# Seven half-size products for u and z of a gMLP layer, sums of weights on GpSimd, y kept where v was

## The chip, the cores and the metric

The kernel runs on one core of one Trainium2 chip. The metric is the device time of one execution in microseconds (us). A core has a matrix engine (TensorE, PE in the profile; its loads of stationary operands are PEld), a vector engine (VectorE, DVE), a scalar engine (ScalarE, ACT), GpSimd (POOL), and queues that start DMA transfers (here almost all on SyncE, SP). Each engine takes its instructions in a fixed order and waits on semaphores for the others.

## The reference, cut to what matters

Two layers work on 512 prompt rows and 128 sample rows (640 tokens, five tiles of 128). Layer 0 is a gMLP, layer 1 an attention layer; after each stand an output product, a norm and a gated embedding. The change is in the gMLP:

```
def gmlp_branch(h, w_in, ln_g, ln_b, w_s, b_s, w_out):
    proj = h @ w_in                      # 640 x 1024 times 1024 x 6144
    uv = gelu(proj[..., :2 * E])         # E = 2048
    z = proj[..., 2 * E:]
    u = uv[..., :E]
    v = layer_norm(uv[..., E:], ln_g, ln_b)
    s = einsum('gij,bnjgc->bnigc', masked w_s, v blocks) + b_s     # 16 groups of 128 columns
    y = u * s * silu(z)
    return y @ w_out, v
```

Everything is float32.

## The kernel before, in words

Every float32 operand of a large product is split in two (`split`): `hi` is a rounded copy made by ScalarE, `lo = x - hi` is made by VectorE. A product is then three matmuls, `mm3`: hi·hi, hi·lo, lo·hi. The input h (normed, transposed) lies split in the tile `A`, as `h_hi` and `h_lo`, eight blocks k of 128 rows by 640 tokens.

Weights come in units of 512 KB, 128 x 1024 on chip. `fetch` starts their DMA into one of three slots of `RAW`; `prefetch` splits a unit into one of five slots of `W`; `weights(n)` hands out the next n units and lets `prefetch` run as far ahead as slots allow. A unit's split waits until the matmuls that read its slot's old content are done.

The gMLP has two stages. The **v stage** makes v token-major: four panels p of 512 columns, in each four units, five token tiles. ScalarE applies the gelu to each bank of PSUM and VectorE gathers the statistics (`bn_stats`). `layer_norm_panel(p)` then takes two VectorE operations for each of five tiles. The **u/z stage** goes through 16 groups g of 128 channels, channel-major. For each pair of groups one weight pair gives u and one gives z: `channel_unit` runs over the eight k, each with two pieces of tokens (384 and 256) of three matmuls. ScalarE takes u out of PSUM with a gelu; z goes through a tanh on ScalarE and one VectorE operation. Then come, for each group, the gate `tz = 0.5 * tz * u`, the weights of the spatial product (`spatial_weights`: a multiply on VectorE, two transposes, three copies on ScalarE), the spatial matmuls on v, two additions of the bias on VectorE out of PSUM, and `y = s * tz`. All eight PSUM banks go round in one ring.

The output product (`tail`) splits y and runs over units of `w_out`.

The program order below is only a proposal: a scheduler at compile time sets each engine's order from its own estimate of when work is ready. Work that is written later can stand earlier on an engine.

Of the kernel before, what the change touches and what calls it, by code (L numbers as in the profile page):

```python
# [10 lines left out]
F32 = mybir.dt.float32  # L14
# [6 lines left out]
P = 128  # L21
# [5 lines left out]
NB = 8  # L27
# [26 lines left out]
def hybrid_trunk(tc, x_prompt, x_sample, ck, cv, clf, p_prompt, p_sample, norm_pre, norm_post,  # L54
# [56 lines left out]
    def dma(out, in_):  # L111
        nc.sync.dma_start(out=out, in_=in_)
# [30 lines left out]
    u_tail(f_wout, 1)  # L143


    n0 = 48 + 16 + 2 + 8
    few = range(n0, n0 + 64 + 12)
    slots, last_use = {}, [-1] * NW
    state = {"raw": 0, "used": 0}

    def raw_of(i):
        o = (i % NRAW) * 1024
        return RAW[:, o:o + 1024]

    def fetch(upto):
        while state["raw"] < min(upto, len(units)):
            ap, k = units[state["raw"]]
            dma(raw_of(state["raw"]).rearrange("p (k n) -> p k n", k=k), ap)
            state["raw"] += 1

    def prefetch(upto, i0=0):

        while len(slots) < min(upto, len(units)):
            i = len(slots)
            taken = {slots[k] for k in range(i0, i)}
            free = [z for z in range(NW - (i in few)) if z not in taken]
            if not free:
                return
            z = min(free, key=lambda z: last_use[z])
            slots[i], last_use[z] = z, i  # L170
            fetch(i + 1)
            split(W[:, z * 2048:z * 2048 + 1024], W[:, z * 2048 + 1024:z * 2048 + 2048], raw_of(i))

    def weights(n):

        i0 = state["used"]
        state["used"] += n
        prefetch(i0 + NW, i0)
        res = []
        for i in range(i0, i0 + n):  # L180
            k, o = units[i][1], slots[i] * 2048
            res.append(tuple(W[:, o + z:o + z + 1024].rearrange("p (k n) -> p k n", k=k) for z in (0, 1024)))
        return res

    def mm3(out, lhs, rhs, start, stop):
        (lh, ll), (rh, rl) = lhs, rhs
# [76 lines left out]
    def channel_unit(ws, hh, banks):  # L263
        return run(channel_steps(ws, hh, banks))

    def interleave(steps, pieces):

# [52 lines left out]
        prefetch(t + 1)  # L320


    def v_at(p, t):
        return r1(p * 2560 + t * 512, 512)

    stats = [small(24, keep=True) for _ in range(NT)]
    for p in range(4):
        out = [bank((0, 1, 2, 3, 4, 5, 6, 7)) for _ in range(NT)]
        for kk in range(4):
            (w,) = weights(1)  # L330
            for t in range(NT):
                for j in range(2):
                    k = 2 * kk + j
                    mm3(out[t], h_at(k, t * P, (t + 1) * P), (w[0][:, j], w[1][:, j]), k == 0, k == 7)
        for t in range(NT):
            nc.scalar.activation(out=v_at(p, t), in_=out[t], func=AF.Gelu_apprx_tanh)
            nc.vector.bn_stats(out=stats[t][:, 6 * p:6 * p + 6], in_=v_at(p, t))
    for p in range(4):
        dma(r2(6144 + p * 1024, 512), ln_g[0, p * 512:(p + 1) * 512].partition_broadcast(P))
        dma(r2(6144 + p * 1024 + 512, 512), ln_b[0, p * 512:(p + 1) * 512].partition_broadcast(P))  # L340
    mu, rs = [], []
    for t in range(NT):
        mv = small(2, keep=True)
# [15 lines left out]
    w16 = r1(o_A, 256).rearrange("p (g j) -> p g j", g=16)  # L359
    for b in range(NB):  # L360
        dma(w16[b * TS:(b + 1) * TS], w_s[0, :, :TS, :TS].rearrange("g i j -> i g j"))
    for z in range(2):
        nc.gpsimd.memset(r1(o_wm + z * P, P)[64:128, 0:64], 0.0)

    def spatial_weights(g):
# [7 lines left out]
        b = bank()  # L373
# [12 lines left out]
    for g in range(16):
        if g == 0:
            layer_norm_panel(2)
        if g == 2:
            layer_norm_panel(3)  # L390
        if g % 2 == 0:
            wz = weights(2)
            for i in range(2):
                for (a, b), o in zip(SPLITS, channel_unit(wz, i, (0, 1, 2, 3, 4, 5, 6, 7))):
                    nc.scalar.activation(out=uv_of(g + i)[0][:, a:b], in_=o[:, :b - a], func=AF.Gelu_apprx_tanh)
            wz = weights(2)
# [14 lines left out]
        nc.tensor.matmul(b1[:, :P], v_at(pnl, 4)[:, c0:c0 + P], ws, start=True, stop=True)  # L411
        nc.vector.tensor_tensor(
            out=tmp[:, :512].rearrange("p (t i) -> p t i", t=4), in0=b0.rearrange("p (t i) -> p t i", t=4),
            in1=bs.unsqueeze(1).broadcast_to([P, 4, P]), op=ALU.add)
        nc.vector.tensor_tensor(
            out=tmp[:, 512:].rearrange("p (t i) -> p t i", t=NB), in0=b1[:, :P].rearrange("p (t i) -> p t i", t=NB),
            in1=bs[:, :TS].unsqueeze(1).broadcast_to([P, NB, TS]), op=ALU.add)
        nc.vector.tensor_tensor(out=tmp, in0=tmp, in1=tz, op=ALU.mult)


    def tail(layer, y_at, first_banks, attention=None):
# [541 lines left out]
```

## Time and profile before

| | |
|---|---|
| three timed runs | 1358.04, 1358.42, 1358.46 us (median 1358.42) |
| profiled execution | 1358.35 us, its span 1356.5 us |
| TensorE busy | 1345.5 us, 99% of the span |
| VectorE busy | 661.0 us, 49% |
| ScalarE busy | 492.1 us, 36% |
| GpSimd busy | 33.6 us, 2% |
| DMA | 170.73 MB, mean 126 GB/s |

The span is what the trace covers; 1.85 us of the execution lie around it. A busy share is a mean over stages with different limits. A matmul's duration in the trace is longer than its distance to the next one, since matmuls are pipelined; the distance from start to start is what counts. The u/z stage lies between about 126 and 373 us.

### The profile page before, as it was taken

What the parts mean: (1) busy time and instruction counts of PE and PEld (TensorE: products, weight loads), DVE (VectorE), ACT (ScalarE), POOL (GpSimd) and SP (SyncE); (2) the same over time, 40 slices, a digit from 0 to 9 for tenths busy, and PEclk for the clock granted to TensorE, in tenths of its full rate; (3) what the DMA queues carried; (4) which work ended last, traced back from release to release, by engine and by line L of the source; (5) the groups of instructions that cost most, each with busy time, mean ns of one, the idle gap of its engine ahead of it and who ended that gap; (6) DMA issues with size and microseconds to landing.
All of it is one profiled execution on the core that took longest, in us unless ns stands there. A gap on an engine that the chain in (4) does not pass through costs nothing.

```text
span 1356.5 us, 21525 instructions
## 1 busy us (share of the span) xinstructions
PE 1345.5 (99%) x8553; PEld 1221.1 (90%) x8553; DVE 661.0 (49%) x1435; ACT 492.1 (36%) x954; POOL 33.6 (2%) x80
## 2 busy tenths in 40 slices
PE   8999999999999999999999999999999999999998
PEld 6888999999988878899999999999999999788786
DVE  7335833343454364644545444554545465544642
ACT  5232222222335343533333333333433344445331
POOL 1000000000000010100000000000000000000100
PEclk8999999999999999999999999999999999999999
DMA  8322332322232213578888676775888587444111
GB/s 280 126 78 65 117 108 80 132 72 73 65 110 78 79 45 83 146 168 164 145 143 173 151 156 153 164 161 126 137 153 171 144 205 225 132 124 132 63 62 47
DMA packets 296983, 170.73 MB, mean 126 GB/s; under 512 B 188450, under 2 KB 266786, under 8 KB 296883
## 3 DMA queue, kind: packets, MB, share of 16 engines
q1 hardware_dynamic: 296738, 169.10, 50.2%
q8 instruction: 67, 1.10, 0.3%
q14 instruction: 34, 0.27, 0.1%
q10 hardware_dynamic: 144, 0.26, 0.1%
HBM read 147.75 MB, written 21.58 MB: 125 GB/s over the span
## 4 chain that ended last, share of the span: by engine, by line
PE 98%; DVE 1%; DMA 0%; ACT 0%; issue 0%; SPq 0%; POOL 0%; DVEq 0%
PE pb L187 29%; PE pb L189 29%; PE pb L188 29%; PE pb L778 3%; PE pb L771 1%; PE pb L832 1%; PE pb L225 1%; PE pb L858 1%; PE pb L410 1%; PE pb L855 1%; DMA RAW<-in_gmlp_w_in 0%; PE pb L850 0%; PE pb L411 0%; PE pb L749 0%; PE pb L865 0%
## 5 line engine op out<-in xcount | busy, mean ns | idle before, releaser
L187 PE MATMUL pb<-A,W 128*128 128x256 f32 (+1 forms) x1280 | 410.3, 321 | 0.0
L189 PE MATMUL pb<-A,W 128*128 128x256 f32 (+1 forms) x1280 | 397.0, 310 | 0.0
L188 PE MATMUL pb<-A,W 128*128 128x256 f32 (+1 forms) x1280 | 395.9, 309 | 0.0
L202 DVE TENSOR_TENSOR W<-RAW,W 128x1024 fp32r<-128x1024 f32 x164 | 200.4, 1222 | 255.2 <-ACT W L201 253.3
L187 PE MATMUL pb<-W,A 128*128 128x512 f32 (+1 forms) x840 | 297.8, 355 | 3.6 <-ACT A L201 2.2
L189 PE MATMUL pb<-W,A 128*128 128x512 f32 (+1 forms) x840 | 293.4, 351 | 0.3 <-DVE A L202 0.3
L188 PE MATMUL pb<-W,A 128*128 128x512 f32 (+1 forms) x840 | 293.6, 350 | 0.0
L201 ACT ACTIVATE W<-RAW 128x1024 fp32r<-128x1024 f32 x164 | 173.0, 1055 | 209.9 <-PE pb L188 106.2
L187 PEld LDWEIGHTS pb<-A,W 128*128 128x128 f32 x1280 | 241.5, 189 | 7.5 <-issue 6.8
L188 PEld LDWEIGHTS pb<-A,W 128*128 128x128 f32 x1280 | 241.3, 189 | 0.6
L189 PEld LDWEIGHTS pb<-A,W 128*128 128x128 f32 x1280 | 240.9, 188 | 0.5 <-issue 0.4
L187 PEld LDWEIGHTS pb<-W,A 128*128 128x128 f32 x840 | 159.0, 189 | 27.6 <-issue 3.1
L189 PEld LDWEIGHTS pb<-W,A 128*128 128x128 f32 x840 | 158.9, 189 | 20.9 <-DVE A L202 0.7
L188 PEld LDWEIGHTS pb<-W,A 128*128 128x128 f32 x840 | 159.0, 189 | 20.2 <-issue 0.4
L810 DVE STREAM_TRANSPOSE r2b_t<-r2b_t 128x256 f32<-128x256 f32 x128 | 46.0, 411 | 30.0 <-PE pb L832 26.7
L773 ACT ACTIVATE R<-pb 128x128 f32<-128x128 f32 (+1 forms) x64 | 28.0, 437 | 65.8 <-PE pb L771 65.6
L202 DVE TENSOR_TENSOR A<-r2a_t,A 128x640 fp32r<-128x640 f32 x32 | 25.0, 821 | 45.3 <-ACT A L201 45.2
L778 PE MATMUL pb<-R 128*128 128x128 f32 x320 | 46.2, 275 | 0.0
L778 PEld LDWEIGHTS pb<-R 128*128 128x128 f32 x320 | 41.5, 191 | 0.8 <-issue 0.4
L201 ACT ACTIVATE A<-r2a_t 128x640 fp32r<-128x640 f32 x32 | 22.7, 740 | 47.4 <-PE pb L188 46.7
L712 DVE SCALAR_TENSOR_TENSOR R<-R,pb 128x384 f32<-128x384 f32 (+1 forms) x32 | 14.8, 484 | 44.5 <-ACT R L711 44.4
L211 POOL TENSOR_TENSOR SML<-SML 128x1 f32<-128x1 f32 x25 | 19.3, 770 | 694.0 <-DVE SML L209 579.4
(198 smaller groups left out, 1386.5 us busy)
## 6 DMA issues: line engine op xcount, KB each, us to landing
RAW<-in_fox_w_in SPq DMA_DIRECT2D x64, 512.0 KB
RAW<-in_gmlp_w_in SPq DMA_DIRECT2D x48, 512.0 KB
r2b_t<-in_cache_fox_v SPq DMA_DIRECT2D x32, 512.0 KB
r2b_t<-in_cache_fox_k SPq DMA_DIRECT2D x128, 128.0 KB
RAW<-in_gmlp_w_out SPq DMA_DIRECT2D x16, 512.0 KB
RAW<-in_ple_w_gate SPq DMA_DIRECT2D x16, 512.0 KB
RAW<-in_fox_w_out SPq DMA_DIRECT2D x16, 512.0 KB
out<-R SPq DMA_DIRECT2D x40, 128.0 KB
```

What stands on the lines that cost most here:

```text
L187: nc.tensor.matmul(out, lh, rh, start=start, stop=False)
L188: nc.tensor.matmul(out, lh, rl, start=False, stop=False)
L189: nc.tensor.matmul(out, ll, rh, start=False, stop=stop)
L201: nc.scalar.activation(out=hi, in_=src, func=AF.Copy)
L202: nc.vector.tensor_tensor(out=lo, in0=src, in1=f(hi), op=ALU.subtract)
L211: nc.gpsimd.tensor_tensor(out=q, in0=t, in1=mhalf, op=ALU.pow)
L225: nc.tensor.transpose(out=b[:, j * P:(j + 1) * P], in_=src[:, (4 * c + j) * P:(4 * c + j + 1) * P], identity=ident)
L410: nc.tensor.matmul(b0[:, t * P:(t + 1) * P], v_at(pnl, t)[:, c0:c0 + P], wm, start=True, stop=True)
L712: nc.vector.scalar_tensor_tensor(out=tz[:, a:b], in0=tz[:, a:b], scalar=1.0, in1=ps[:, :b - a], op0=ALU.add, op1=ALU.mult)
L773: nc.scalar.activation(out=pt[:, :n], in_=tb[:, :n], func=AF.Copy)
L778: nc.tensor.matmul(O[:, d], v[:, j, hh * P:(hh + 1) * P], pt[:, j * P:(j + 1) * P], start=(j == 0), stop=(j == i))
L810: nc.vector.transpose(out=kt[:, hh, bl, :PAST], in_=kr[:, hh, bl])
```

## The change

u and z of a pair of groups (256 channels by 640 tokens, 1024 deep) are no longer made by eight half-size products (two halves of channels, two of tokens, two of depth) but by seven, in Strassen's way (Winograd's form). A half-size product has 128 channels, 320 tokens and a depth of 512: four k, three matmuls each, 12 matmuls.

- **Right operands** (from h): four sums of quarters of h. `right_operands` makes them once, on VectorE, in the v stage: four additions hi + lo and four subtractions of 128 x 1280, and three splits into a new tile `TB`; the fourth is split into the place of a quarter of h that nothing reads after (`split(*quarter(0, 1), b12)`).
- **Left operands** (from weights): `left_operands` makes four sums of quarters of the two weight units, 128 x 512 each, on GpSimd, into the tile `SF`, which has room for one set. So each set of seven needs four splits in place of two: one of 512 columns and three of 1024. `W` is handed out in ten half slots. A fourth slot for raw weights (`o_X`) is added.
- **Results**: `seven_products` puts each product into one of four banks (`UZ`); the other four (`SPA`) serve the spatial part. One product is copied by ScalarE; each of the other six is taken out of PSUM by VectorE additions, seven in all for each set (L485, L495, L497, L500). The gelu and the tanh then read SBUF.
- **y in place of v**: y of group g is written over the columns of v that it was made from (`y0_at`); the place that y had is used by `TB` and `SF`. Gain and bias of the layer norm are loaded panel by panel into one place (`load_ln`), and the norm of panels 1 to 3 is written between the groups.

```
+    def left_operands(i, j):
+        (a11, a21), (a12, a22) = ([raw_of(r).rearrange("p (k n) -> p k n", k=4)[:, :, z:z + P] for z in (0, P)] for r in (i, i + 1))
+        s2, s3, s1, s4 = (SF[:, z * 512:z * 512 + 512].rearrange("p (k n) -> p k n", k=4) for z in range(4))
+        if j == 0:
+            for o, a, b, op in ((s1, a21, a22, ALU.add), (s2, s1, a11, ALU.subtract), (s3, a11, a21, ALU.subtract),
+                                (s4, a12, s2, ALU.subtract)):
+                nc.gpsimd.tensor_tensor(out=o, in0=a, in1=b, op=op)
+        return (a11, SF[:, :1024], SF[:, 1024:2048], raw_of(i + 1))[j]
...
+    def right_operands():
+        for q, (i, j) in zip((b11, b12, b21, b22), ((0, 0), (0, 1), (1, 0), (1, 1))):
+            hi, lo = quarter(i, j)
+            nc.vector.tensor_tensor(out=q, in0=f(hi), in1=f(lo), op=ALU.add)
+        for o, a, b, dst in ((t_a, b12, b11, 0), (t_b, b22, t_a, 1), (b21, b21, t_b, 2), (b12, b22, b12, None)):
+            nc.vector.tensor_tensor(out=o, in0=a, in1=b, op=ALU.subtract)
+            if dst is not None:
+                split(*right_sum(dst), o)
...
+            if (p, kk) == (0, 1):
+                right_operands()
+            if (p, kk) == (3, 1):
+                split(*quarter(0, 1), b12)
...
+    UZ = (0, 1, 2, 3)
+    def seven_products(into, done):
+        rights = (quarter(0, 0), right_sum(1), quarter(0, 1), right_sum(0), quarter(1, 1), quarter(1, 0), right_sum(2))
+        def total(i, j, a, b):
+            nc.vector.tensor_tensor(out=into(i, j), in0=a, in1=b, op=ALU.add)
+            done(i, j, into(i, j))
+        for n, (w, right) in enumerate(zip(seven_left(), rights)):
+            o = bank(UZ)[:, :HT]
+            for k in range(4):
+                mm3(o, (w[0][:, k], w[1][:, k]), (right[0][:, k], right[1][:, k]), k == 0, k == 3)
+            if n == 0:
+                nc.scalar.activation(out=m1, in_=o, func=AF.Copy)
+            elif n == 1:
+                nc.vector.tensor_tensor(out=u2, in0=m1, in1=o, op=ALU.add)
+            elif n == 2:
+                nc.vector.tensor_tensor(out=u3, in0=u2, in1=o, op=ALU.add)
+            elif n == 3:
+                total(1, 1, u3, o)
+                nc.vector.tensor_tensor(out=u2, in0=u2, in1=o, op=ALU.add)
+            elif n == 4:
+                total(0, 1, u2, o)
...
-        tmp = r2(g * TOK, TOK)
-        for (a, b), o in zip(SPLITS, channel_unit(wz, g % 2, (0, 1, 2, 3, 4, 5, 6, 7))):
-            nc.scalar.activation(out=tz[:, a:b], in_=o[:, :b - a], func=AF.Tanh, scale=0.5)
-            nc.vector.scalar_tensor_tensor(out=tz[:, a:b], in0=tz[:, a:b], scalar=1.0, in1=o[:, :b - a], op0=ALU.add, op1=ALU.mult)
...
+    for g in range(0, 16, 2):
+        for part, finish in ((0, finish_u), (1, finish_z)):
+            if 2 * part in SEVEN:
+                seven_products(lambda i, j: uv_of(g + i)[part][:, HALF[j]], lambda i, j, c: finish(g, i, j, c))
+            else:
+                eight_products(lambda i, j, c: finish(g, i, j, c))
+        if g < 12:
+            layer_norm_panel(1 + g // 4, range(3) if g % 4 == 0 else range(3, NT))
+        for i in range(2):
+            gate_spatial(g + i)
```

What the change does to the order of the engines shows at the beginning of the u/z stage. On VectorE before, at the first groups of z, stand the last operations of the layer norm (L352, L353), the tanh's product that frees a bank of z (L401), splits of weights (L202) and the spatial part (L370, L412, L415); `pb_71` is PSUM bank 1, `R_69` the tile that holds v, u, tz and the rest.

```order
L353 SCALAR_TENSOR_TENSOR R_69<-R_69,SML,r2a_t 128x512 x2
L401 SCALAR_TENSOR_TENSOR R_69<-R_69,pb_71 128x384
L353 SCALAR_TENSOR_TENSOR R_69<-R_69,SML,r2a_t 128x512
L401 SCALAR_TENSOR_TENSOR R_69<-R_69,pb_72 128x256
L370 TENSOR_TENSOR R_69<-CST,R_69 128x128
L202 TENSOR_TENSOR W<-RAW,W 128x1024
L401 SCALAR_TENSOR_TENSOR R_69<-R_69,pb_76 128x384
```

On VectorE now, at the end of the first set of seven (u of groups 0 and 1) and the start of the second, the sums that free the four banks (L485, L500) stand between the layer norm of panels 1 and 2 (L435, L436), the bias additions of the first groups (L525, L527) and splits (L251).

```order
L251 TENSOR_TENSOR W<-RAW,W 128x1024
L435 SCALAR_TENSOR_TENSOR R_69<-R_69,SML 128x512 x5
L485 TENSOR_TENSOR R_69<-R_69,pb_73 128x320
L500 TENSOR_TENSOR R_69<-R_69,pb_73 128x320
L485 TENSOR_TENSOR R_69<-R_69,pb_71 128x320
L458 TENSOR_TENSOR R_69<-CST,R_69 128x128
L525 TENSOR_TENSOR R_69<-pb_76,R_69 128x4x128
L525 TENSOR_TENSOR R_69<-pb_75,R_69 128x4x128
L436 SCALAR_TENSOR_TENSOR R_69<-R_69,SML 128x512 x2
L485 TENSOR_TENSOR R_69<-R_69,pb_72 128x320
```

In the program panel 1 is normed after the sets of u and z; on VectorE its five first operations now stand ahead of the sums of the fourth product (bank 3, rows three and four), and so ahead of the release of the banks that the second set needs.

On GpSimd before, nothing but the small powers of the norms (L211) stands here. Now the sums of weights (L185) of the second and third set stand around the five powers of the layer norm (L260).

```order
L185 TENSOR_TENSOR sf<-R_69 128x512 [waits DMAHW6_49,DVE_49]
L185 TENSOR_TENSOR sf<-R_69,RAW 128x512 [waits DMAHW6_49,DMAHW3_49,DVE_49]
L185 TENSOR_TENSOR sf<-sf,R_69 128x512 [waits Pool_49]
L185 TENSOR_TENSOR sf<-RAW,sf 128x512 [waits Pool_49]
L260 TENSOR_TENSOR SML<-SML 128x1 [waits DVE_49] x3
L185 TENSOR_TENSOR sf<-RAW 128x512 [waits DMAHW7_49,DVE_49]
L260 TENSOR_TENSOR SML<-SML 128x1 [waits DVE_49] x2
L185 TENSOR_TENSOR sf<-RAW 128x512 [waits DMAHW1_49,DVE_49]
```

The last two powers, which the norm of tiles 3 and 4 needs, now stand behind a sum that waits for a split on VectorE.

## Rows read from the trace of the kernel before

**Rows 1.** Profile page: span, busy times, the chain that ended last.
```profile
span 1356.5 us, 21525 instructions
...
PE 1345.5 (99%) x8553; PEld 1221.1 (90%) x8553; DVE 661.0 (49%) x1435; ACT 492.1 (36%) x954; POOL 33.6 (2%) x80
...
PE 98%; DVE 1%; DMA 0%; ACT 0%; issue 0%; SPq 0%; POOL 0%; DVEq 0%
```
**Rows 2.** Windows: us, busy us (instructions) of PE, PEld, DVE, ACT, POOL, granted clock, DMA.
```profile
0.00:36.00 36.00, 31.48 (x133) 23.84 (x134) 25.82 (x52) 18.05 (x30) 3.98 (x11) 0.91 0.85 285
36.00:126.00 90.00, 90.00 (x399) 74.53 (x398) 30.48 (x36) 25.16 (x31) 0.99 (x1) 1.00 0.29 92
126.00:373.00 247.00, 247.00 (x1720) 246.91 (x1719) 120.61 (x190) 70.82 (x149) 3.94 (x4) 1.00 0.28 89
```
**Rows 3.** Windows of 10 and 20 us in the u/z stage; VectorE third.
```profile
126.00:136.00 10.00, 10.00 (x69) 9.91 (x68) 10.00 (x20) 2.96 (x7) 0.99 (x1) 1.00 0.03 8
...
156.00:166.00 10.00, 10.00 (x76) 10.00 (x75) 9.09 (x17) 2.74 (x7) 0.00 (x0) 1.00 0.68 230
...
286.00:306.00 20.00, 20.00 (x140) 20.00 (x140) 5.32 (x9) 4.95 (x11) 0.00 (x0) 1.00 0.20 62
```
**Rows 4.** Timeline of PE, u/z stage's start and middle: start, us, instruction.
```profile
126.33 0.42 PE L187 MATMUL pb<-A,W 128*128 128x384 f32 x1
...
302.68 0.27 PE L374 MATMUL pb<-CST,R 128*128 128x128 f32 x1
...
303.93 0.42 PE L187 MATMUL pb<-A,W 128*128 128x384 f32 x1
...
304.89 0.33 PE L187 MATMUL pb<-A,W 128*128 128x384 f32 x1
...
308.42 0.34 PE L187 MATMUL pb<-A,W 128*128 128x384 f32 x1
```
**Rows 5.** Groups by line and form, VectorE: count, busy us, mean ns.
```profile
L202 DVE TENSOR_TENSOR W<-RAW,W 128x1024 fp32r<-128x1024 f32 x164 | 200.4, 1222 | 255.2 <-ACT W L201 253.3 <-DMA out<-R 0.5
...
L202 DVE TENSOR_TENSOR W<-R,W 128x512 fp32r<-128x512 f32 x32 | 21.9, 686 | 0.4 <-ACT W L201 0.4
...
L353 DVE SCALAR_TENSOR_TENSOR R<-R,SML,r2a_t 128x512 f32<-128x512 f32 x20 | 13.9, 744 | 0.0
...
L402 DVE SCALAR_TENSOR_TENSOR R<-R 128x640 f32<-128x640 f32 x16 | 13.1, 820 | 0.2
...
L401 DVE SCALAR_TENSOR_TENSOR R<-R,pb 128x384 f32<-128x384 f32 x16 | 8.8, 548 | 4.9 <-ACT R L400 4.9
...
L401 DVE SCALAR_TENSOR_TENSOR R<-R,pb 128x256 f32<-128x256 f32 x16 | 6.6, 412 | 0.0
```
**Rows 6.** Timeline of VectorE and GpSimd where both are at work.
```profile
5.48 0.56 POOL L211 TENSOR_TENSOR SML<-SML 128x1 f32<-128x1 f32 x1 [4.51 <-DVE SML L209]
...
123.60 2.73 DVE L352 SCALAR_TENSOR_TENSOR R<-R,SML,r2a_t 128x512 f32<-128x512 f32 x4
...
123.77 0.99 POOL L211 TENSOR_TENSOR SML<-SML 128x1 f32<-128x1 f32 x1 [97.64 <-DVE SML L207]
...
486.37 1.21 DVE L202 TENSOR_TENSOR W<-RAW,W 128x1024 fp32r<-128x1024 f32 x1
486.53 1.48 POOL L211 TENSOR_TENSOR SML<-SML 128x1 f32<-128x1 f32 x1 [2.93 <-DVE SML L209]
...
648.22 0.22 POOL L825 TENSOR_TENSOR R<-R,CST 128x16 f32<-128x16 f32 x1 [11.54 <-DMA R<-cs_sc]
```
**Rows 7.** Groups by line and form, GpSimd.
```profile
L659 POOL MEMSET R<- 128x1024 f32 x1 | 1.0, 967 | 5.4 <-DVE R L535 5.4
L363 POOL MEMSET R<- 64x64 f32 x2 | 0.2, 146 | 0.3 <-POOLq L950 0.3
```
**Rows 8.** Timeline of VectorE while h is made, with its waits.
```profile
30.43 1.29 DVE L202 TENSOR_TENSOR A<-pb,A 128x512 fp32r<-128x512 f32 x2 [0.53 <-ACT A L201]
...
35.41 0.69 DVE L202 TENSOR_TENSOR A<-pb,A 128x512 fp32r<-128x512 f32 x1 [0.65 <-ACT A L201]
```

More of the change, by code (lines that the diff above doesn't have):

```diff
@@ L143, in hybrid_trunk @@
     u_tail(f_wout, 1)
-    n0 = 48 + 16 + 2 + 8
+    S0, S1 = 16, 48
+    SEVEN = (0, 2)
+    items = []
+    for i in range(len(units)):
+        if not S0 <= i < S1 or i % 4 - i % 2 not in SEVEN:
+            items.append((i, None))
+        elif i % 2 == 0:
+            items += [(i, j) for j in range(4)]
+    n0 = S1 + 16 + 2 + 8
     few = range(n0, n0 + 64 + 12)
-    slots, last_use = {}, [-1] * NW
+    place, last_use = [], [-1] * (2 * NW)
     state = {"raw": 0, "used": 0}
     def raw_of(i):
-        o = (i % NRAW) * 1024
-        return RAW[:, o:o + 1024]
+        if S0 <= i < S1:
+            z = (i - S0 + 1) % 4
+            if z == NRAW:
+                return r1(o_X, 1024)
+        else:
+            z = i % NRAW if i < S0 else (i + 1) % NRAW
+        return RAW[:, z * 1024:z * 1024 + 1024]
     def fetch(upto):
@@ L159, in fetch @@
             state["raw"] += 1
-    def prefetch(upto, i0=0):
[L163 to L166, printed above, removed]
+    def left_operands(i, j):
[6 more added lines that the diff above has]
+        return (a11, SF[:, :1024], SF[:, 1024:2048], raw_of(i + 1))[j]
+    def prefetch(upto, i0=0):
+        while len(place) < min(upto, len(items)):
+            i = len(place)
+            u, j = items[i]
+            taken = {z for k in range(i0, i) for z in place[k]}
+            step = 1 if j == 0 else 2
+            free = [z for z in range(0, 2 * (NW - (u in few)), step) if not taken & set(range(z, z + step))]
             if not free:
                 return
[L169 to L172, printed above, removed]
+            z = min(free, key=lambda z: max(last_use[z:z + step]))
+            place.append(range(z, z + step))
+            last_use[z:z + step] = [i] * step
+            fetch(u + 1 if j is None else u + 2)
+            o, n = z * 1024, step * 512
+            hi, lo = W[:, o:o + n], W[:, o + n:o + 2 * n]
+            if j is None:
+                split(hi, lo, raw_of(u))
+            else:
+                split(*((x.rearrange("p (k n) -> p k n", k=4) for x in (hi, lo)) if j == 0 else (hi, lo)), left_operands(u, j))
+                if u > S0:
+                    fetch(u + 4)
     def weights(n):
@@ L177, in weights, with seven_left @@
         state["used"] += n
-        prefetch(i0 + NW, i0)
+        prefetch(i0 + 2 * NW, i0)
         res = []
         for i in range(i0, i0 + n):
-            k, o = units[i][1], slots[i] * 2048
-            res.append(tuple(W[:, o + z:o + z + 1024].rearrange("p (k n) -> p k n", k=k) for z in (0, 1024)))
-        return res
+            u, j = items[i]
+            k, o, m = units[u][1], place[i][0] * 1024, len(place[i]) * 512
+            if j in (1, 2):
+                views = [W[:, o + z:o + z + m].rearrange("p (a k n) -> p k a n", a=2, k=k) for z in (0, m)]
+            else:
+                views = [W[:, o + z:o + z + m].rearrange("p (k n) -> p k n", k=k) for z in (0, m)]
+            res.append(tuple(views))
+        return res
+    def seven_left():
+        for j in range(4):
+            (w,) = weights(1)
+            for a in range(1 if j == 0 else 2):
+                yield tuple(z[:, :, a] if j in (1, 2) else z[:, :, a * P:(a + 1) * P] for z in w)
     def mm3(out, lhs, rhs, start, stop):
@@ L243, in hybrid_trunk, with channel_steps @@
     SPLITS = ((0, SA), (SA, TOK))
-    def channel_steps(ws, hh, banks):
+    def channel_steps(ws, hh, banks, splits=SPLITS):
         out = [bank(banks), bank(banks)]
@@ L249, in channel_steps @@
             w = [z[:, k % 4, hh * P:(hh + 1) * P] for z in ws[k // 4]]
-            for (a, b), o in zip(SPLITS, out):
+            for (a, b), o in zip(splits, out):
                 mm3(o[:, :b - a], w, h_at(k, a, b), k == 0, k == 7)
@@ L263, in channel_unit @@
     def channel_unit(ws, hh, banks):
[L264 removed]
+        return run(channel_steps(ws, hh, banks, ((0, TOK // 2), (TOK // 2, TOK))))
     def interleave(steps, pieces):
@@ L320, in hybrid_trunk, with quarter, right_sum @@
         prefetch(t + 1)
+    o_X, o_ln, o_sum, o_th = 14208, 15232, 16256, 17216
+    HT = TOK // 2
+    pool2.release()
+    pool2 = tc.alloc_tile_pool(name="r2t", bufs=1, reuse_waits="tile")
+    TB = pool2.tile([P, 7680], F32R, name="tb")
+    SF = pool2.tile([P, 2560], F32, name="sf")
+    def quarter(i, j):
+        return tuple(z[:, 4 * i:4 * i + 4, j * HT:(j + 1) * HT] for z in (h_hi, h_lo))
+    def right_sum(i):
+        return tuple(TB[:, z:z + 4 * HT].rearrange("p (k n) -> p k n", k=4) for z in (i * 2560, i * 2560 + 1280))
+    b11, b12, b21, b22, t_a, t_b = (r1(10240 + z * 1280, 1280).rearrange("p (k n) -> p k n", k=4) for z in (0, 1, 2, 3, 4, 0))
+    def right_operands():
[6 more added lines that the diff above has]
+                split(*right_sum(dst), o)
     def v_at(p, t):
@@ L378, in spatial_weights, with y0_at @@
         nc.scalar.activation(out=ws, in_=b[:, P:2 * P], func=AF.Copy)
-    layer_norm_panel(0)
-    layer_norm_panel(1)
-    spatial_weights(0)
     def uv_of(g):
         return r1(o_u + (g % 2) * TOK, TOK), r1(o_tz + (g % 2) * TOK, TOK)
[L386 to L396, printed above, removed]
+    def y0_at(g):
+        return r1(g // 4 * 2560, 2560).rearrange("p (t n) -> p t n", t=NT)[:, :, (g % 4) * P:(g % 4 + 1) * P]
@@ new lines, in hybrid_trunk @@
+    m1, u2, u3 = (r1(o_sum + z * HT, HT) for z in range(3))
+    HALF = (slice(0, HT), slice(HT, TOK))
+    UZ = (0, 1, 2, 3)
[19 more added lines that the diff above has]
+                total(0, 1, u2, o)
+            elif n == 5:
+                total(0, 0, m1, o)
+            else:
+                total(1, 0, u3, o)
@@ L397, in hybrid_trunk, with eight_products, gate_spatial @@
+    def eight_products(done):
+        wz = weights(2)
+        for i in range(2):
+            for j, o in enumerate(channel_unit(wz, i, UZ)):
+                done(i, j, o[:, :HT])
+    def gate_spatial(g):
         u, tz = uv_of(g)
[L398 to L401 removed]
@@ L457, in split_y @@
             while ready < min(upto, 32):
-                split(y_part(ready, 0), y_part(ready, 1), y_at(ready % 16, ready // 16))
+                y, parts = y_at(ready % 16, ready // 16), (y_part(ready, 0), y_part(ready, 1))
+                split(*(parts if last else (x.rearrange("p (t n) -> p t n", t=NT) for x in parts)), y)
                 ready += 1
```

53 lines of the change are left out of this document (35 added, 18 removed).

## Prediction, written before the changed kernel ran

> **What bounds the kernel now.** The page comes first [rows 1]: PE is busy for 99% of the span, and the chain that ended last is 98% PE. The windows say that this holds in the stage that is changed: from 126 to 373 us PE is busy for all of 247.0 us at the full granted clock, and VectorE for 120.6 us [rows 2]. Fewer matmuls there shorten the span by their whole distance, as long as nothing else begins to wait. The finer windows show where that could end: VectorE is full in the stage's first 10 us and still busy for 9.1 of the 10 from 156 us, and later falls to a quarter (5.3 of 20 us from 286) [rows 3]. That full stretch is the layer norm of all of v beside the first groups. PE does not feel it before, since u leaves PSUM through ScalarE, eight banks go round, and weights lie up to four units ahead. So the reader is to keep three engines in view: PE, VectorE, and GpSimd, which has 33.6 us of work in all.
>
> **Matmuls removed.** There are 16 sets (eight pairs of groups, u and z). Each drops from 96 matmuls to 84, of 320 columns now, and of 384 and 256 (mean 320) before. From 304.89 to 308.42 us lie four steps of k, 24 matmuls [rows 4]: 0.147 us each. 16 x 12 x 0.147 = **-28.2 us**. A product of 12 is 1.76 us, a set 12.35 us. The spatial part of a group (two transposes and five matmuls) takes 1.25 us, 302.68 to 303.93 [rows 4], as before.
>
> **VectorE at the stage's beginning.** Now each set's sums stand on VectorE, and PE is at most four products ahead of them (four banks). The order of the changed kernel has 122 VectorE operations from the first of the layer norm to just ahead of the first sum of the fourth set: 40 of the layer norm (0.744), ten splits of 1024 (1.222), four of 512 (0.686), 25 operations of 320 columns (21 sums, four of the tanh; 0.48, the mean of 548 and 412 ns), nine bias additions of 512 (0.686), 19 of 128 columns (0.28, the 256-column price less the step from 384 to 256), four of 640 (0.82), and 11 small ones (3.2 us) [rows 5]. That makes 29.8 + 12.2 + 2.7 + 12.0 + 6.2 + 5.3 + 3.3 + 3.2 = 74.7 us. Back to back they overlap a little: four of the norm take 2.73 us, not 2.98 [rows 6], 0.08 less each; 122 x 0.08 = 9.8. About 65 us are left. They begin some 2.7 us ahead of the stage (before, the norm at 123.60 [rows 6] and the first matmul of u at 126.33 [rows 4]), so PE has 62 us to fill. It has 21 products of three sets and, going by which banks are free by then, one of the fourth: 38.8 us; and the spatial part of nine groups that the order puts there, 11.3 us. **PE waits 12 us** (14 with no product of the fourth set, 7 with all four). It doesn't get them back: behind it PE itself is the limit.
>
> **Sums of weights on GpSimd.** No row has a GpSimd operation of this size. Its fill of 1024 elements takes 0.967 us and of 64 0.146 [rows 7]: 0.86 ns an element. 512 elements in one pass would be 0.6 us, in three passes (two reads, a write) 1.5. I take two passes, 0.88, and the 0.22 of a 16-element addition [rows 6]: 1.1 us. A set's four take 4.4 us, beside the 12.35 of PE; its place is free once the last set's splits are done, and the order splits a set ahead. GpSimd alone does not bound.
>
> But the two engines get in each other's way. A GpSimd power takes 0.56 us, but 0.99 when a layer norm operation runs on VectorE, and 1.48 when a 1024-column split does: each time it ends about 0.4 us after that VectorE operation's end [rows 6]. Both of those read two operands in SBUF. That GpSimd holds VectorE up in turn is not shown, since a power reads one element a lane; the four norm operations around it kept their pace. Bounds: 0, or 1.1 us for each of the 12 sums that fall into the full stretch, 13 us. By the order eight of the 12 come where VectorE's next operations read two SBUF operands (norm, splits, gates), not PSUM. I take **9 us**: two operations that exclude each other one way most likely do so the other way.
>
> The Trainium skill, page "SBUF — State Buffer", section "Who interferes with whom", states that a VectorE instruction with two SBUF inputs contends with a GpSimd instruction that reads SBUF, and that the second to issue blocks until the first has finished. The half of it that rows can show agrees (1.48 for 0.56 us). By it alone all 12 would count, 13 for 9 us. Its page "GPSIMD Engine Reference", section "Performance versus the Vector engine", gives 4497 ns for an addition of 2048 elements; a quarter is an estimate of 1.12 us.
>
> **The later sets.** For a pair of groups VectorE then has six splits of 1.222, two of 0.686, 18 operations of 320 columns, four of 640: 20.6 us, less 30 x 0.08, 18.2, against 24.7 of PE. Splits lie a set ahead. 6.5 us are free; if all eight GpSimd sums (8.8) pushed VectorE, PE would wait 2.3 us for each of about four pairs. Bounds 0 and 10, I take **2**: sums read PSUM, and much of GpSimd's work falls beside them or into VectorE's waits.
>
> **The v stage.** Four additions, four subtractions and three splits of 1280 columns (1.49 each, by the slope from 512 to 1024 columns) are 16.4 us of VectorE, which is busy for 30.5 of the 90 us from 36 on [rows 2]. But two or three of them stand ahead of the splits of token tile 4, where VectorE before waits only 0.53 and 0.65 us [rows 8]. Tile 4 comes 0 to 4 us later, and PE's order gives it matmuls right then: **2 us**.
>
> **ScalarE and the rest.** ScalarE gets one and a half 1024-column splits and a copy more for a set (it is busy for 70.8 of 247 us [rows 2]); PE's loads of stationary operands keep their number per matmul. DMAs of weights are the same bytes; the new norm loads stand on SP ahead of raw units that are used a set later. The end of the stage frees h's first half four products early. I put these at 0. Where PE waits for several us, its granted clock may fall: in the first 36 us, with 4.5 us of waits, it was 0.91 [rows 2], between the levels of 1.2 and 2.4 GHz. Most of the loss falls into time in which PE would wait again. Bounds 0 and 6; **2 us**.
>
> **Sum.** 1356.5 - 28.2 + 12 + 9 + 2 + 2 + 2 = 1355.3; with the 1.85 us around the span, 1357.2, say **1357 us**. The profiled execution (1358.35) is the median of the runs (1358.42) within 0.1. I take 0.2% (2.7 us) as what can be told from no change.
>
> **Rivals.**
> 1. *GpSimd does not hold VectorE.* For it: the norm's pace beside a power. Against: the power itself waits. The 9 us and most of the later 2 fall away: 1347 us. Chance 0.25.
> 2. *VectorE's backlog is hidden too*, because PE finds enough spatial work, or VectorE runs faster than its rows. Against: 62 us stand against at most 55. Only the v stage and some collisions stay: 1333 to 1341 us. Chance 0.07.
> 3. *Slower: VectorE becomes the bound of the later sets.* If GpSimd pushes it for all of 8.8 us in a pair, VectorE needs 27 us where PE needs 24.7. It decides from 6.5 us of pushing a pair. With all 12 sums counted in the stretch (+4) and 10 for 2 later: 1369 us, and up to 1377 if the clock falls too. For it: of the 20.6 us of a pair 13.9 (splits, gates, the tanh's product) read two SBUF operands. By the skill's rule above this is possible, not forced, as GpSimd can use the gaps. Chance 0.18.
> 4. *The forecast*, backlog and collisions costing about what the products save: 1350 to 1366 us. Chance 0.5.
>
> **How the numbers follow.** The range leaves out rival 2 and the far end of rival 3: 1343 to 1371. The forecast's own is 1350 to 1366. Faster than 1355.7: rival 4 gives 0.14, rival 1 0.21, rival 2 0.07: 0.42. Within 2.7 us: 0.18 + 0.03 = 0.21. Slower: 0.18 + 0.18 and 0.01 of rival 1: 0.37.
>
> **What the profile after would show.** PE's 320-column matmuls start 0.147 us apart, 192 fewer in the stage. The windows of the stage's first 75 us show VectorE full and PE with some 20 us idle, put down to the sums (L485, L495, L497) and to banks 0 to 3; later windows show PE full. GpSimd's sums last 1.1 us alone and up to 2.3 beside splits; additions of the norm beside them last longer than 0.744. I am wrong if PE is full from the stage's start (rival 2), if the norm keeps its 0.744 us beside GpSimd (rival 1), or if PE waits as much after the first 75 us as before (rival 3).

## The result, and the profile after

The changed kernel takes 1347.51 us (median of four runs, 1346.84 to 1347.90), the kernel before 1358.44 beside it: a ratio of 0.9919 [0.9902, 0.9936], faster by 0.8%. The forecast was 1357 us, the range 1343 to 1371. The side and the range hold; the number is 9.5 us too high, and the time is that of the first rival, though not for that rival's reason.

The profile page after (span, busy times, the chain that ended last) answers to [rows 1]:

```profile
span 1345.1 us, 21508 instructions
...
PE 1323.2 (98%) x8361; PEld 1196.4 (89%) x8361; DVE 777.5 (58%) x1591; ACT 532.6 (40%) x1006; POOL 136.7 (10%) x144
...
PE 96%; DVE 2%; issue 1%; DMA 0%; ACT 0%; SPq 0%; POOL 0%; DVEq 0%; ACTq 0%
```

There are 192 matmuls fewer (8361 for 8553), VectorE has 116.5 us more to do and GpSimd 103. VectorE now stands in the chain. The windows after, with the columns of [rows 2], say where:

```profile
36.00:126.00 90.00, 90.00 (x401) 74.51 (x400) 44.48 (x52) 30.07 (x37) 13.10 (x12) 1.00 0.34 98
126.00:206.00 80.00, 67.16 (x446) 65.75 (x445) 77.13 (x126) 30.68 (x68) 27.98 (x20) 0.91 0.31 95
206.00:346.00 140.00, 140.00 (x973) 139.99 (x972) 127.10 (x181) 66.43 (x114) 66.93 (x41) 1.00 0.27 85
...
136.00:146.00 10.00, 6.53 (x46) 6.14 (x45) 10.00 (x14) 2.52 (x6) 5.19 (x3) 0.91 0.58 191
146.00:156.00 10.00, 10.00 (x57) 10.00 (x55) 10.00 (x16) 1.98 (x5) 1.74 (x1) 0.75 0.22 70
...
166.00:176.00 10.00, 5.35 (x27) 5.36 (x28) 10.00 (x16) 2.30 (x5) 2.71 (x2) 0.66 0.34 105
```

All of PE's idle time in the stage lies in its first 80 us, where VectorE is full; from 206 us on PE is full although VectorE is busy for 127.1 of 140 us. The timeline of PE names the waits (those with a bracket; the rows between show the pace):

```profile
125.89 0.39 PE L236 MATMUL pb<-A,W 128*128 128x320 f32 x1
...
126.70 0.31 PE L238 MATMUL pb<-A,W 128*128 128x320 f32 x1
126.85 0.31 PE L236 MATMUL pb<-A,W 128*128 128x320 f32 x1
...
141.90 1.16 PE L522 MATMUL pb<-R 128*128 128x128 f32 x8 [1.13 <-ACT R L466]
145.40 0.63 PE L236 MATMUL pb<-A,W 128*128 128x320 f32 x1 [2.34 <-DVE R L500]
...
146.10 0.47 PE L238 MATMUL pb<-A,W 128*128 128x320 f32 x1
146.36 0.47 PE L236 MATMUL pb<-A,W 128*128 128x320 f32 x1
...
160.43 1.16 PE L522 MATMUL pb<-R 128*128 128x128 f32 x8 [0.96 <-ACT R L466]
170.65 0.79 PE L523 MATMUL pb<-R 128*128 128x128 f32 x2 [7.30 <-DVE R L525]
...
187.47 1.16 PE L522 MATMUL pb<-R 128*128 128x128 f32 x8 [0.98 <-ACT R L466]
...
362.60 0.48 PE L236 MATMUL pb<-W,A 128*128 128x512 f32 x1
```

Five waits make 12.7 us. Behind the two long ones the matmuls start 0.26 us apart (146.10 to 146.36) in place of 0.15 (126.70 to 126.85): the granted clock is 0.75 and 0.66 in those windows, between the levels of 1.2 and 2.4 GHz. The stage lasts from 125.89 to 362.60, 236.7 us; before it lasted 248.5 (126.33 [rows 4] to the first matmul of the output product at 374.80). So it is 11.8 shorter where the products alone give 28.2: TensorE loses 16.4 us, 12.7 in waits and the remaining 3.7 at the lower clock (29 starts some 0.267 us apart, 145.83 to 150.90 and 171.93 to 174.60, are 3.5 us by themselves). The stage begins 0.4 us earlier, and what follows it lasts 0.8 longer (1345.1 - 362.6 against 1356.5 - 374.8). -11.8 - 0.4 + 0.8 is the span's -11.4.

Does GpSimd hold VectorE up? The timeline of both engines after the change:

```profile
117.39 1.28 POOL L185 TENSOR_TENSOR sf<-sf,R 128x512 f32<-128x512 f32 x1
...
130.12 1.66 POOL L185 TENSOR_TENSOR sf<-RAW 128x512 f32<-128x512 f32 x1 [1.51 <-DVE W L251]
130.55 1.78 DVE L436 SCALAR_TENSOR_TENSOR R<-R,SML 128x512 f32<-128x512 f32 x1
...
137.53 1.60 POOL L185 TENSOR_TENSOR sf<-sf,RAW 128x512 f32<-128x512 f32 x1
137.92 2.29 DVE L251 TENSOR_TENSOR W<-RAW,W 128x1024 fp32r<-128x1024 f32 x1
139.21 2.14 POOL L185 TENSOR_TENSOR sf<-RAW,sf 128x512 f32<-128x512 f32 x1
...
163.59 0.74 DVE L436 SCALAR_TENSOR_TENSOR R<-R,SML 128x512 f32<-128x512 f32 x1
163.74 1.70 POOL L185 TENSOR_TENSOR sf<-R,RAW 128x512 f32<-128x512 f32 x1 [10.40 <-DVE W L251]
164.25 5.75 DVE L435 SCALAR_TENSOR_TENSOR R<-R,SML 128x512 f32<-128x512 f32 x4
165.52 1.59 POOL L185 TENSOR_TENSOR sf<-sf,R 128x512 f32<-128x512 f32 x1
167.19 1.59 POOL L185 TENSOR_TENSOR sf<-RAW,sf 128x512 f32<-128x512 f32 x1
169.92 0.68 DVE L525 TENSOR_TENSOR R<-pb,R 128x512 f32<-128x512 f32 x1
```

It does. A sum lasts 1.28 us while VectorE is still (117.39). At 130.55 a norm operation of 0.74 us takes 1.78, at 137.92 a split of 1.22 takes 2.29, and four norm operations that took 2.73 before [rows 6] take 5.75 beside three sums. The first two end 0.55 and 1.08 us after the sum beside them, as if most of the operation had begun only then. Behind the third block stands what ends the longest wait: the bias addition (169.92) frees the bank of the spatial part for which PE stands from 163.35 to 170.65, with the next products behind it in its queue. (Without the sums this wait is 5.0 us, so that they make the smaller part of it.) By groups, for VectorE from 120 to 205 us after the change:

```profile
L435 DVE SCALAR_TENSOR_TENSOR R<-R,SML 128x512 f32<-128x512 f32 x20 | 18.6, 974 | 0.0
L436 DVE SCALAR_TENSOR_TENSOR R<-R,SML 128x512 f32<-128x512 f32 x20 | 15.9, 823 | 0.0
...
L251 DVE TENSOR_TENSOR W<-RAW,W 128x1024 fp32r<-128x1024 f32 x5 | 7.6, 1530 | 4.3 <-ACT W L250 4.2
L485 DVE TENSOR_TENSOR R<-R,pb 128x320 f32<-128x320 f32 x14 | 6.6, 474 | 0.0
```

The norm's operations last 974 and 823 ns on the mean in place of 744 [rows 5], splits of raw weights 1530 for 1222; the sums out of PSUM last 474, between the 412 and 548 of 256 and 384 columns [rows 5].

### The profile page after: what moved, and what is told of

It reads as the page before. It is cut to its first block, busy times and chain, and to the rows that moved or that the text cites. A ratio compares the mean times of both kernels' runs of the same rounds, so it can differ in the third digit from the quotient of the medians.

```text
span 1345.1 us, 21508 instructions
## 1 busy us (share of the span) xinstructions
PE 1323.2 (98%) x8361; PEld 1196.4 (89%) x8361; DVE 777.5 (58%) x1591; ACT 532.6 (40%) x1006; POOL 136.7 (10%) x144
## 4 chain that ended last, share of the span: by engine, by line
PE 96%; DVE 2%; issue 1%; DMA 0%; ACT 0%; SPq 0%; POOL 0%; DVEq 0%; ACTq 0%
PE pb L236 29%; PE pb L238 28%; PE pb L237 28%; PE pb L915 3%; PE pb L908 1%; PE pb L969 1%; PE pb L274 1%; PE pb L995 1%; DVE R L435 1%; PE pb L522 1%; DVE R L436 1%; PE pb L992 1%; DVE W L251 0%; PE pb L987 0%; DMA RAW<-in_gmlp_w_in 0%
## 5 line engine op out<-in xcount | busy, mean ns | idle before, releaser
L236 PE MATMUL pb<-A,W 128*128 128x384 f32 (+2 forms) x1024 | 331.2, 323 | 2.3 <-DVE R L500 2.3
L238 PE MATMUL pb<-A,W 128*128 128x384 f32 (+2 forms) x1024 | 318.5, 311 | 0.0
L237 PE MATMUL pb<-A,W 128*128 128x384 f32 (+2 forms) x1024 | 317.5, 310 | 0.0
L236 PE MATMUL pb<-W,A 128*128 128x512 f32 (+1 forms) x840 | 298.2, 355 | 2.1 <-ACT R L641 1.4
L251 DVE TENSOR_TENSOR W<-RAW,W 128x1024 fp32r<-128x1024 f32 (+1 forms) x156 | 194.0, 1245 | 151.4 <-ACT W L250 149.1
L250 ACT ACTIVATE W<-RAW 128x1024 fp32r<-128x1024 f32 (+1 forms) x156 | 161.2, 1033 | 168.0 <-PE pb L237 74.9
L236 PEld LDWEIGHTS pb<-A,W 128*128 128x128 f32 x1024 | 194.0, 189 | 10.0 <-issue 6.8
L237 PEld LDWEIGHTS pb<-A,W 128*128 128x128 f32 x1024 | 194.0, 189 | 0.6
L238 PEld LDWEIGHTS pb<-A,W 128*128 128x128 f32 x1024 | 193.6, 189 | 0.4 <-issue 0.4
L236 PEld LDWEIGHTS pb<-W,A 128*128 128x128 f32 x840 | 159.0, 189 | 26.2 <-issue 3.1
L251 DVE TENSOR_TENSOR A<-R,A 128x640 fp32r<-128x640 f32 (+1 forms) x51 | 41.0, 835 | 74.6 <-ACT A L250 72.3
L250 ACT ACTIVATE A<-R 128x640 fp32r<-128x640 f32 (+1 forms) x51 | 36.7, 748 | 67.7 <-PE pb L237 65.7
L236 PE MATMUL pb<-tb,W 128*128 128x320 f32 x192 | 60.6, 316 | 0.0
L237 PE MATMUL pb<-tb,W 128*128 128x320 f32 x192 | 59.8, 312 | 0.0
L238 PE MATMUL pb<-tb,W 128*128 128x320 f32 x192 | 59.8, 312 | 0.0
L260 POOL TENSOR_TENSOR SML<-SML 128x1 f32<-128x1 f32 x25 | 19.2, 769 | 387.5 <-DVE SML L258 380.7
```

What stands on the lines that cost most here:

```text
L236: nc.tensor.matmul(out, lh, rh, start=start, stop=False)
L237: nc.tensor.matmul(out, lh, rl, start=False, stop=False)
L238: nc.tensor.matmul(out, ll, rh, start=False, stop=stop)
L260: nc.gpsimd.tensor_tensor(out=q, in0=t, in1=mhalf, op=ALU.pow)
```

## The experiments

Each ran beside the kernel before, whose median was 1358.1 to 1358.3 us in every set. Medians are of four runs or more.

**The sums left out.**

```
-        if j == 0:
+        if False:
             for o, a, b, op in ((s1, a21, a22, ALU.add), ...
-        return (a11, SF[:, :1024], SF[:, 1024:2048], raw_of(i + 1))[j]
+        return (a11, raw_of(i), raw_of(i), raw_of(i + 1))[j]
```

> Left out: the 64 sums of weights on GpSimd; the splits read the raw weights in their place, as many and as large, so that u and z come out of unsummed weights. VectorE keeps its order. Theory A (sums hold VectorE up): the changed kernel's trace has VectorE operations of 0.74 us that last 1.78, and of 1.21 that last 2.29, beside a sum; up to 176 us they add some 7 us, which reach TensorE. Without sums the norm keeps 0.74 us everywhere and the time falls to 1340.5 us (1339 to 1343). Rival B (only the backlog of the layer norm makes TensorE wait, sums fall into slack): 1347 us, no change. Rival C (the sums make all of the wait): some 1331 us.

Measured: 1340.73 us, 0.9869 [0.9853, 0.9886] of before; 6.8 us less than the changed kernel. The same two groups of the norm, in its trace:

```profile
L436 DVE SCALAR_TENSOR_TENSOR R<-R,SML 128x512 f32<-128x512 f32 x20 | 14.3, 742 | 0.0
L435 DVE SCALAR_TENSOR_TENSOR R<-R,SML 128x512 f32<-128x512 f32 x20 | 14.0, 742 | 0.0
```

and PE's waits from 120 to 400 us (what was waited for: us in all, times, longest):

```profile
PE pb L523 <- DVE R L525: 5.0, 1, 5.0
PE pb L522 <- ACT R L466: 3.0, 3, 1.1
```

VectorE does the same 1591 operations in 751.5 us in place of 777.5. So theory A holds and B and C fall: the sums cost VectorE 26 us in all and the kernel 6.8, and without them a loss remains. The stage is 229.1 us long here (126.36 to 355.42), 8.8 above the 220.3 (248.5 - 28.2) that the fewer products alone would leave.

**The sums on VectorE.**

```
-                nc.gpsimd.tensor_tensor(out=o, in0=a, in1=b, op=op)
+                nc.vector.tensor_tensor(out=o, in0=a, in1=b, op=op)
```

> The same 64 sums of weights, on VectorE instead of GpSimd: none beside another engine's, but 0.61 us each back to back on VectorE (the addition of 512 columns, 0.69, less overlap). Theory A (a sum on GpSimd costs VectorE about as much as the sum itself would there): 12 sums in the full stretch cost 7.3 us in place of 7, later pairs have 18.2 + 4.9 = 23.1 of 24.7 us, still hidden: 1346 to 1350 us. Rival B (sums on GpSimd cost nothing): 7 us more than the changed kernel, 1354 us or above.

Measured: 1346.93 us, 0.9916 [0.9901, 0.9930], the changed kernel's time within 0.6, as theory A has it; B falls. By groups, a sum there and a norm operation:

```profile
L185 DVE TENSOR_TENSOR sf<-RAW 128x512 f32<-128x512 f32 x16 | 10.9, 684 | 7.3 <-DMA RAW<-in_gmlp_w_in 7.3
...
L435 DVE SCALAR_TENSOR_TENSOR R<-R,SML 128x512 f32<-128x512 f32 x20 | 14.0, 744 | 0.0
```

Nothing is drawn out, and nothing is won: VectorE is busy for 785.3 us in all, for 777.5 with the sums on GpSimd. Handing 64 sums to the idle engine saved the busy one 8 us out of 34.

**The norm kept in its written place.** The last line holds an instruction behind all that is written ahead of it on its engine.

```
+            for s, o, op0, op1 in ((mu[t], o_ln, ALU.subtract, ALU.mult), (rs[t], o_ln + 512, ALU.mult, ALU.add)):
+                x = nc.vector.scalar_tensor_tensor(out=v, in0=v, scalar=s, in1=r1(o, 512), op0=op0, op1=op1)
+                if p:
+                    tc.keep_in_program_order(x)
```

> The layer norm of panels 1 to 3 keeps its written place on VectorE, behind what is written ahead of it; no operation is added or removed. The changed kernel's TensorE loses 16.4 us between 126 and 199 us (12.7 of waits, the rest at a lower clock). Theory A (the order puts the norm ahead of the sums that free banks): the waits go, 1333 to 1338 us, and VectorE, which has some 10% free from 205 us on, takes the norm there. Rival D (the amount of VectorE's work decides, not the order): the waits move to the later sets, 1343 to 1348 us.

Measured: 1352.80 us, 0.9959 [0.9944, 0.9974]: slower than the changed kernel by 5.3, outside both expectations. PE's waits from 120 to 400 us (line numbers are higher by two here: L502 is L500, L525 is L523, and L436 the norm):

```profile
PE pb L236 <- DVE R L502: 11.7, 7, 3.0
PE pb L525 <- DVE R L436: 2.7, 2, 1.4
PE pb L524 <- DVE R L436: 1.0, 2, 0.5
PE pb L236 <- DVE R L499: 0.3, 1, 0.3
```

The waits are 15.7 us, more than the changed kernel's 12.7, in twelve places along the whole stage instead of five at its beginning: they moved, as rival D has it, and grew. The granted clock is 0.83 to 0.94 in four windows of 10 us (from 196, 206, 266 and 326 us). Theory A was wrong here: moving the norm doesn't make it smaller, and a block of four or six norm operations behind a set stands near the next set's sums. Two of them, drawn out beside GpSimd, stand right ahead of L487 and L502, for which PE waits until 171.29:

```profile
166.99 3.46 DVE L436 SCALAR_TENSOR_TENSOR R<-R,SML 128x512 f32<-128x512 f32 x2
```

**The norm left out for four of five tiles.**

```
         for t in tiles:
+            if p and t < 4:
+                continue
```

> Left out: the layer norm of panels 1 to 3 for the four tiles of prompt rows, 24 VectorE operations; sums of weights stay on GpSimd. Theory A (VectorE's backlog, norm and collisions together, makes all of the 16.4 us that TensorE loses): 24 operations at 0.66 us back to back are 15.8 us less, and the sums that met them meet nothing; VectorE then needs about 55 us where TensorE has 57: 1331 to 1334 us. Rival F (four banks, the chain of sums and splits, or the spatial part hold TensorE up whatever VectorE's load): 1340 us or more.

Measured: 1333.55 us, 0.9820 [0.9806, 0.9835], as theory A has it; F falls. PE waits 2.9 us in the stage, which lasts 223.1 (126.36 to 349.42), 2.8 above the products alone. With four banks, the chain of sums and splits and the spatial part all as they were, it is the amount of VectorE's work at the beginning that costs; the order alone, moved above, gave nothing back.

**No sets of seven.**

```
-    SEVEN = (0, 2)
+    SEVEN = ()
```

> Eight half-size products again in place of seven, without sums of weights; all else of the change stays (y in place of v, norm panel by panel, right operands made in the v stage; the eight products read one of these in place of a quarter of h, so that u and z come out of other numbers). Theory A: the rest of the change costs nothing, TensorE has no waits in the stage: 1357 to 1359 us. Rival E (the rest of the change costs several us by itself, as the v stage's 2 us in the forecast): 1361 us or more.

Measured: 1357.17 us, 0.9992 [0.9983, 1.0001]; PE has no wait in the stage. Theory A holds and E falls: the rest of the change costs nothing that can be told. The products alone, from here to the norm left out, are worth 23.6 us with 2.9 of waits and some lower clock (0.93 and 0.90 from 136 to 156 us) still in them, in keeping with 28.2. One thing shows here that the accounts by 248.5 - 28.2 leave out: the stage lasts 246.4 us (126.45 to 372.81), 2.1 less than before with as many products. Of these, 0.6 are six transposes (L442) that stood just ahead of the output product before and come after its start now, which is most of the 0.8 by which the rest lasts longer; the other 1.5 have no row. Counted from 246.4, every loss against the products alone would be 2.1 us larger.

**More work on VectorE in the later sets.** From the third pair on, the split's subtraction is made again, for the third of a set's four splits, or for the second and third.

```
+                if u >= S0 + 8 and j in (2,):        # the second kernel: (1, 2)
+                    nc.vector.tensor_tensor(out=lo, in0=left_operands(u, j), in1=f(hi), op=ALU.subtract)
```

> From the third pair of groups on, one subtraction of 1024 columns on VectorE in each set is made twice, two for a pair (the values don't change). The changed kernel's VectorE is busy for 127.1 of the 140 us from 206 on, so about 2.3 us are free in a pair of 24.7. Two more of 1.13 us back to back take just these. Theory A (a pair's slack on VectorE is what hides sums and collisions): 1347 to 1351 us. Rival H (there is no usable slack, the chain of sums, splits and banks already stands at its limit): 2.3 us for each of six pairs, 1361 us.

> The same with two subtractions in each set, four for a pair: 4.5 us where 2.3 are free. Theory A: VectorE becomes the bound of the later sets, 2.2 us more for each of six pairs, 1361 us (1357 to 1366). Rival I (collisions give way when VectorE is full, so that there is more slack than the busy time shows): 1350 us or less.

Measured: 1355.18 us, 0.9978 [0.9968, 0.9987], and 1361.84, 1.0027 [1.0017, 1.0037]. Four more: theory A, within a microsecond, and rival I falls. Two more: between A and H, 7.7 us or 1.3 a pair where A allowed 0 to 4 in all. For two more, PE's waits from 206 to 390 us, the window 206 to 346, and VectorE's splits from 206 to 346 (L497 is L495, L253 the split):

```profile
PE pb L238 <- DVE R L497: 6.3, 4, 1.7
```
```profile
206.00:346.00 140.00, 133.65 (x922) 132.60 (x921) 131.06 (x177) 60.57 (x106) 64.69 (x41) 1.00 0.26 81
```
```profile
L253 DVE TENSOR_TENSOR W<-sf,W 128x1024 fp32r<-128x1024 f32 x20 | 25.0, 1251 | 8.2 <-ACT W L252 8.2
```

VectorE reaches 131 of 140 us and PE waits already; 8.2 of the 9 us left end with ScalarE's half of a split, and so weren't VectorE's to use. So the changed kernel's later sets stand close to the edge.

**The norm on ScalarE, a version that beats both.**

```
+            if t < 4:
+                nc.scalar.activation(out=v, in_=v, func=AF.Identity, scale=rs[t], bias=shift[t])
+                continue
...
+        nc.tensor.matmul(b1[:, P:2 * P], CST[:, C_TRI + 384:C_TRI + 512], wm, start=True, stop=True)
...
-            out=y[:, :4], in0=b0.rearrange("p (t i) -> p t i", t=4), in1=bs.unsqueeze(1).broadcast_to([P, 4, P]), op=ALU.add)
+        nc.vector.scalar_tensor_tensor(out=bs, in0=b1[:, P:2 * P], scalar=bcol[:, g:g + 1], in1=bs, op0=ALU.mult, op1=ALU.add)
+        nc.vector.scalar_tensor_tensor(
+            out=y[:, :4], in0=b0.rearrange("p (t i) -> p t i", t=4), scalar=gcol[:, g:g + 1],
+            in1=bs.unsqueeze(1).broadcast_to([P, 4, P]), op0=ALU.mult, op1=ALU.add)
```

The columns 384 to 511 of that constant are all ones, so the extra matmul gives the row sums of the masked weights, which carry the norm's bias.

> Nothing left out: the norm of the four prompt tiles is one ScalarE operation (scale 1/sigma, shift -mu/sigma), and gain and bias of each channel come in the spatial part, where a channel is a partition: one more matmul of 128 columns and one more VectorE operation of 128 columns for a group. VectorE loses 32 operations of 0.66 us (21.1) and gets 16 of 0.28; ScalarE gets 16 of 512 columns. Theory A: TensorE's 16.4 us of loss go, less 16 matmuls of some 0.11 us: 1332 to 1335 us. Rival G (ScalarE, which frees banks too, becomes the late one in the full stretch): 1338 us or more.

Measured: 1337.90 us, 0.9850 [0.9833, 0.9866]: 9.6 below the changed kernel, 3 above theory A's end, at the edge of rival G. PE's waits, the new ScalarE operation (L441) and the added matmul (L532, which runs in two passes; L531 is the matmul of L523, L538 the bias addition, L493 a sum):

```profile
PE pb L531 <- DVE R L538: 1.6, 1, 1.6
PE pb L530 <- ACT R L441: 1.2, 1, 1.2
PE pb L236 <- DVE R L493: 1.0, 1, 1.0
```
```profile
L441 ACT ACTIVATE R<-R,SML 128x512 f32<-128x512 f32 x16 | 11.7, 802 | 0.0
```
```profile
215.19 0.39 PE L532 MATMUL pb<-R,CST 128*128 128x128 f32 x2
215.41 0.27 PE L470 MATMUL pb<-CST,R 128*128 128x128 f32 x1
```

The stage lasts 227.2 us (126.50 to 353.72), 6.9 above the products alone. The 16 added matmuls take 3.5 of these: each is two passes, 0.22 us from its start to the next, and the expectation had counted one of some 0.11. Mending that alone moves theory A's end to some 1337, and so most of its miss was this count. Of the 16.4 us some 3.4 are left, in keeping with 3.8 of waits; 1.2 of them are ScalarE's, which G would have, and the larger part is still VectorE's.

## Why the prediction was right, and where it was off

**The matmuls, -28.2: right.** 192 fewer, 0.147 us apart (126.70 to 126.85); what the stage didn't give back is found in PE's waits and clock.

**VectorE's backlog, +12 (7 to 14), and the clock, +2: the mechanism right, the size too large.** VectorE is full from 123 to 195 us, and without the sums TensorE still loses 8.8 us, clock included, for the 14 forecast. VectorE's 65 us were right: without the sums it is busy for 65.3 from the norm's first operation to the fourth set's first sum.

```profile
123.52:192.01 68.49, 60.39 (x413) 58.69 (x412) 65.30 (x124) 28.02 (x64) 5.99 (x5) 0.95 0.39 115
```

The step that failed is the count of what PE can do meanwhile: it gave the fourth set one product. The changed kernel's window up to that sum, for L236 alone, one of three lines of equal count, and the sum itself:

```profile
125.80:199.19 73.39, 33.12 (x97) 19.82 (x97) 0.91 0.33 102
```
```profile
199.19 0.49 DVE L495 TENSOR_TENSOR R<-R,pb 128x320 f32<-128x320 f32 x1 [0.60 <-PE pb L238]
```

3 x 97 matmuls are 24.25 products, 2.25 more than the 22 in the sum: 4.0 us. The lower bound, with all four, was the one to take. The row of the sum says more: there VectorE waits for PE, and not PE for VectorE. The backlog is worked off by then; the last wait put down to VectorE ends at 170.65, after 13 products, and the account should have been made up there and not at the fourth set. The text also looked for some 20 us of idle PE, put down to the sums and to banks 0 to 3. There are 12.7, and only 2.3 of them stand at these banks; 7.3 stand at a bank of the spatial part, whose bias addition is queued behind the same norm, and 3.1 at ScalarE's copies of the spatial weights (L466), for which the sum had nothing. The spatial bank is the same backlog seen from another place. That the copies are too is not shown: with the norm left out their waits are gone and without the sums they stay (3.0), but two of the three copies stand behind a weight's split on ScalarE (at 140.49 and 185.66).

**The sums on GpSimd, +9 (0 to 13): right for VectorE, 1.4 to 2.2 less in time.** VectorE's norm, splits, tanh product and L458 are drawn out by 9.0 us in the full stretch (40 norm operations by 232 and 81 ns on the mean of each half, five splits by 311, three tanh products and eleven operations of L458 by 0.7 and 0.5 us in all, against the kernel without sums); taking the sums away gives 7.6 us in the stage and 6.8 of the whole time. A sum alone takes 1.28 us where the estimate was 1.1. The reason given was the half that [rows 6] show, a power held up by VectorE; the other half is now measured. The Trainium skill, "SBUF — State Buffer", "Who interferes with whom", says that the order of issue decides who blocks, and that a VectorE instruction with at most one SBUF input, outside its two-port modes, doesn't contend. The trace agrees, with 2.29 for 1.22 us where the sum began first and with the PSUM sums' 474 ns (480 without sums on GpSimd). The forecast's 12 full blocks would have been 13 us; some sums begin beside PSUM operations, and 9 it was.

**The later sets, +2 (0 to 10): 0.** PE has no wait in the stage after 188 us. The pushing is there: VectorE is busy for 127.1 us from 206 to 346, 108.3 without the sums, which is 18.8 us or 3.3 a pair. It fell into idle time, as the term allowed. But rival 3's point of 6.5 us a pair was too far: two splits more (3.3 + 2.3 of added work) cost 1.3 a pair, four more (3.3 + 4.5) cost 2.4, so that it decides from some 4.3 to 5.4. The forecast's 18.2 us of VectorE work in a pair had left out four bias additions and two multiplies of spatial weights (some 2 us); without sums 19.1 are measured (108.3 of 140), which leaves 5.6 of 24.7.

**The v stage, +2 (0 to 4): -0.4.** The last split of h ends at 36.8 us, not 36.1 [rows 8], and PE doesn't wait for it; the u/z stage begins at 125.89 for 126.33. In the runs above it begins at 126.36 to 126.71, so that the term is nothing and the 0.4 no gain to count on.

**The sum.** 12 + 9 + 2 were 23 for a loss that is 16.4: 5.2 too much for backlog and clock, 1.4 for collisions. With 2 for the later sets and 2.4 for the v stage, less 0.8 that the rest of the kernel took, this makes the 10.2 between the forecast's span, 1355.3, and 1345.1. **Rival 1** gave 1347 for a GpSimd that does not hold VectorE. It does; the time came there because the other terms were too large, and by its own condition, the norm at 0.744 us beside GpSimd, the rival is refuted. Without collisions the kernel takes 1341. **Rival 2** needed a hidden backlog, and the norm left out shows what that would be: 1333.6, inside its 1333 to 1341. **Rival 3** is refuted as it stands, but is near: 2.3 us more of VectorE work a pair cost time, and with 4.5 more the kernel is slower than before.

What stays open: 1.2 of the 5.2 us above aren't given to a row. They are less than the 2.1 us by which the stage without sets of seven is shorter than before, for which the sum had no term.

## What to carry to other kernels

When an edit moves the release of PSUM banks to an engine, count that engine's backlog at the stage's entry and not its mean share; and count every bank ring that its queue releases, also the ones the edit doesn't touch, since PE issues in order and stands at whichever comes first. Work given to GpSimd is not free for VectorE where VectorE's neighbours read two SBUF operands: here it took the same time as on VectorE itself. What helped here was less work on the full engine: moving the norm to ScalarE won 10 us, and the one other order that was tried, the norm in its written place, lost 5.

## What the runs showed that was not expected

A GpSimd sum lengthens a VectorE operation by most of the sum's own 1.28 us (0.74 by 1.04, 1.22 by 1.07), and is drawn out itself from 1.28 to as much as 2.14 us; over the kernel 64 sums cost VectorE 26 us, 0.41 each. Waits of 2.3 and 7.3 us were each followed by some 4 to 6 us of matmuls at nearly half pace (0.267 us apart for 0.147), some 3.5 us lost on top of 12.7 of waiting. A float32 matmul of 128 columns took two passes, 0.22 us in all.
